# Sample scores of six of eight chains computed inside the next tile's visit, in spare PSUM columns

## The chip, the cores and the metric

The kernel runs on one core of one Trainium2 chip. The metric is the device time of one execution in microseconds (us). TensorE (PE in the profile, its weight loads PEld) multiplies matrices into PSUM, which has eight banks of 512 fp32 columns; VectorE (DVE) and ScalarE (ACT) read PSUM and do the elementwise work; GpSimd (POOL) and SyncE (SP, which issues most transfers) work beside them.

## The reference

One inference step of a two-layer decoder of width 2048: layer 0 is a gated linear recurrence (HGRN2), layer 1 a sliding-window attention with 32 query heads of 64, 4 key heads and a sink per query head. Each layer has an input projection, the mixer with a SiLU gate, an output projection and a LayerNorm. It serves one prompt (16 learned tokens and 256) and 8 samples of 8 tokens, which share the weights. The change touches only the attention of the samples:

```python
keys = jnp.concatenate([cache_k.astype(jnp.float32), k], axis=1)      # 128 cached + 8 own, per sample
s = jnp.einsum('bnqhgd,bnshd->bnhgqs', q, k) * SWA_SCALE
s = jnp.where(mask[None, :, None, None], s, -jnp.inf)
m = jnp.maximum(jnp.max(s, axis=-1, keepdims=True), sink)
p = jnp.exp(s - m)
p = p / (jnp.sum(p, axis=-1, keepdims=True) + jnp.exp(sink - m))
```

## The kernel before

**The stream of projections.** All projections of both layers are one stream of tiles of 128 output columns. A tile has 16 steps of three matmuls: weights are split into a high part (whi, a cast on ScalarE, L170) and a remainder (wlo, a subtraction on VectorE, L181), and each step multiplies low by high, high by low and high by high (L236 to L238). Four steps share one loaded chunk of weights, which is split seven chunks ahead. In layer 1 the stream runs over 2 key tiles, 2 value tiles, 16 query tiles (pj_q), 16 gate tiles (pj_g) and the output projection (y, yr).

**Side work by steps.** Everything else is written as Python generators that run beside the stream while the program is built. After each step `Stream.step` lets at most two waiting generators run on; a generator's `yield n` means: go on n steps later. So the order of instructions on every engine is fixed when the program is built, and a `yield` is a place in the order, not a time. Each engine works through its own list in order.

**A query tile's chain.** When query tile j is projected, `query_chain` undoes the folded LayerNorm (un on VectorE, L930 and L932, then qf on ScalarE, L934), splits the result into qh (ScalarE, L289) and ql (VectorE, L290), copies the samples' part into qs (GpSimd, L1090), waits ten steps and makes visit j.

**A visit.** `visit(n)` first puts on TensorE, without a pause: the prompt's scores of tile n (L1136, tiles sa and sb, from the pool lv that has two banks), the value products of tile n-2 (L1150, tile ao, from the pool mm that has three banks), the samples' value products where they are due (L1157, L1162), the transposes of tile n-1's probabilities (L1169 to L1173, tiles p1 and p2, also mm), and a transpose of cached keys (L1182, ck) or of sample probabilities (L1186, st) where due. One step later it spawns `softmax_chain(n)` and copies what TensorE made out of PSUM on ScalarE (L1194 to L1208). The softmax chain scales and masks the scores on VectorE (sm, L1236), takes the maxima (L1238, L1240) and, in `softmax`, the statistics (L1065 to L1067), three steps later the exponentials on ScalarE (L1070, L1071), and three steps after these the sums and the normalisation on VectorE (L1073 to L1076). Visit n+1 needs its result.

**The samples.** They are done in eight chains (q, u): key head q = 0 to 3, half u of the samples. The table `plan` gives each its visits: with n = 4q + 3 + u, cached keys are loaded in visit n-1 (SP, L1220 and L1223), transposed and copied to kzs in visit n ("keys", L1182 and L1204), and the finished probabilities are transposed in visit n+2 ("trans", L1186) and multiplied with the values in visit n+3 ("out"); for q = 3 the last two are somewhat earlier. In visit n, four steps after the copies (and after the next load, where there is one), `sample_scores` takes two banks of lv (ssa, ssb) and puts 16 small matmuls on TensorE (L1258): per group of 32 rows the 128 cached keys, then the 64 own keys, for each half of the rows. The profile shows each as two. One step later VectorE scales and masks them (sms, L1266), takes the maximum (L1268), and the same `softmax` follows. The scores of the next tile take the same two banks of lv.

Of the kernel before, what the change touches and what calls it, by code (L numbers as in the profile page):

```python
# [21 lines left out]
F32 = mybir.dt.float32  # L22
# [7 lines left out]
P = 128  # L30
D = 2048
KT = D // P
# [218 lines left out]
def hybrid_trunk(tc, x_prompt, x_sample, state_hgrn, cache_k, cache_v, meta, w_in0, lb_logits, norm_w, w_out0,  # L251
                 w_in1, sinks, w_out1, ln_g, ln_b, masks, consts, sinks_s,
                 y_prompt, y_sample, st_p, st_s, kp_out, vp_out, ks_out, vs_out, dbg=None, stage=9):
    nc = tc.nc
# [4 lines left out]
    with es:  # L259
# [9 lines left out]
        lv = pool("lv", 2, space=PSUM)  # L269
# [5 lines left out]
        def pm(name):  # L275
            return mm.tile([P, 512], F32, tag="mm", name=name)
# [665 lines left out]
        L = {"att": 0, "ngate": 0, "nq": 0}  # L942
# [118 lines left out]
        def softmax(stat, parts, sink):  # L1061

            n = len(parts)
            mxs, nmx, sks, rsum = (stat[:, c * n:(c + 1) * n] for c in range(4))
            nc.vector.tensor_tensor(mxs, mxs, sink, op=ALU.max)  # L1065
            nc.vector.tensor_scalar(nmx, mxs, -1.0, None, op0=ALU.mult)
            nc.vector.tensor_tensor(sks, sink, mxs, op=ALU.subtract)  # L1067
            yield 3
            for c, pt in enumerate(parts):
                nc.scalar.activation(pt, pt, AF.Exp, bias=nmx[:, c:c + 1], accum_out=rsum[:, c:c + 1])  # L1070
            nc.scalar.activation(sks, sks, AF.Exp)  # L1071
            yield 3
            nc.vector.tensor_tensor(rsum, rsum, sks, op=ALU.add)  # L1073
            nc.vector.reciprocal(rsum, rsum)
            for c, pt in enumerate(parts):
                nc.vector.tensor_scalar(pt, pt, rsum[:, c:c + 1], None, op0=ALU.mult)  # L1076
# [23 lines left out]
        plan = {}  # L1100
        for q in range(4):
            for u in range(2):
                n = 4 * q + 3 + u
# [9 lines left out]
        def visit(n, qq=None):  # L1113
            ap = L["ap"]
            todo = plan.get(n, {})
# [4 lines left out]
            if n < KT:  # L1120
# [3 lines left out]
                pa = [lv.tile([P, 512], F32, tag="lv", name=f"s{c}{n}") for c in "ab"]  # L1124
                for own in range(2):
                    t0 = 0 if own == 0 else 128
                    for i, (a, b) in enumerate(((ql, kh), (qh, kl), (qh, kh))):
                        for h in range(2):
                            r = halves2[h]
                            if own == 0:  # L1130
                                o, w, ks = (256, 0)[h], 144, b[r, 0:144]
                            elif h == 0:
                                o, w, ks = 0, 256, b[r, :].rearrange("p (a k) -> p a k", a=2)[:, :, 0:128]
                            else:
                                o, w, ks = 144, 256, b[r, 16:272]
                            nc.tensor.matmul(pa[h][:, o:o + w], a[r, t0:t0 + 128], ks, start=i == 0,  # L1136
                                             stop=i == 2, tile_position=(64 * h, 0), skip_group_check=True)
            po = None
            j2 = n - 2
            if j2 >= 0:  # L1140
                po = pm(f"ao{j2}")
            if 0 <= j2 < KT:
                vs = slice(64 * (j2 // 4), 64 * (j2 // 4) + 64)
                t1, t2 = L["t1", j2], L["t2", j2 % 2]
                for v in ("vm1", "vm2", "vm0"):
                    for h in range(2):
                        o, w, l, t = {"vm1": (0, 256, L[v], t1[:, 256 * h:256 * h + 256]),
                                      "vm2": (128, 128, L[v], t2[:, 128 * h:128 * h + 128]),
                                      "vm0": (0, 128, L["vm0"][:, h], t2[:, 256:384])}[v]
                        nc.tensor.matmul(po[halves2[h], o:o + w], l[:, vs], t, start=v == "vm1", stop=v != "vm1",  # L1150
                                         tile_position=(0, 64 * h), skip_group_check=True)
            if "out" in todo:
                q, u = todo["out"]
# [5 lines left out]
                for i in range(4):  # L1159
                    for h in range(2):  # L1160
                        c = 256 * h + 32 * i
                        nc.tensor.matmul(po[halves2[h], 256 + 32 * i:288 + 32 * i], cv[:, i, :], ts[:, c:c + 32],  # L1162
                                         start=False, stop=i == 3, tile_position=(0, 64 * h), skip_group_check=True)
            j = n - 1
            if 0 <= j < KT:
                sm = L["p", j]
                p1, p2 = pm(f"p1_{j}"), pm(f"p2_{j}")
                for h in range(2):
                    nc.tensor.transpose(p1[:, 256 * h:256 * h + 128], sm[:, 256 + 160 * h:384 + 160 * h], ident)  # L1169
                    nc.tensor.transpose(p1[:, 256 * h + 128:256 * h + 256], sm[:, 544 * h:544 * h + 128], ident)  # L1170
                for h in range(2):
                    nc.tensor.transpose(p2[:, 128 * h:128 * h + 128], sm[:, 544 * h + 128:544 * h + 256], ident)
                nc.tensor.transpose(p2[0:32, 256:384], sm[:, 384:416], ident)  # L1173
            px = None
            for kind in ("keys", "trans"):
                if kind in todo:
                    q, u = todo[kind]
# [11 lines left out]
            if n < KT:  # L1189

                g = softmax_chain(n, pa)
                st.spawn(g, next(g))
            if 0 <= j2 < KT:
                nc.scalar.copy(L["oT"][:, j2, 0:256], po[:, 0:256])  # L1194
            if 0 <= j < KT:
# [6 lines left out]
            if "keys" in todo:  # L1202
                q, u = todo["keys"]
# [5 lines left out]
            if "out" in todo:  # L1209
                yield 2  # L1210
                q, u = todo["out"]
# [3 lines left out]
            if "load" in todo:  # L1215
                yield 1 if "out" in todo else 3
                q, u = todo["load"]
# [4 lines left out]
                cv = ap.tile([P, 4, 64], F32, tag="cv", name=f"cv{q}_{u}")  # L1222
                nc.sync.dma_start(cv, cache_v[0, 4 * u:4 * u + 4, :, q, :].rearrange("b s d -> s b d"))  # L1223
                L["cd", u], L["cv", u] = cd, cv
            if "keys" in todo:
                yield 4
                yield from sample_scores(*todo["keys"])

        def softmax_chain(n, pa):
            ap = L["ap"]  # L1230

            sm = ap.tile([P, 1088], F32, tag="sm", name=f"sm{n}")
            stat = ap.tile([P, 16], F32, tag="stat", name=f"stat{n}")
            for h in range(2):
                m0 = 0 if h else 656
                nc.vector.scalar_tensor_tensor(sm[:, 400 * h:400 * h + 400], pa[h][:, 0:400], 0.125,  # L1236
                                               L["cst"][:, m0:m0 + 400], op0=ALU.mult, op1=ALU.add)
            nc.vector.tensor_reduce(stat[:, 0:2], sm[:, 256:544].rearrange("p (h k) -> p h k", h=2), axis=AX.X,  # L1238
                                    op=ALU.max)
            nc.vector.tensor_reduce(stat[:, 2:4], sm.rearrange("p (h k) -> p h k", h=2)[:, :, 0:256], axis=AX.X,  # L1240
                                    op=ALU.max)
            sink4 = ap.tile([P, 2, 2], F32, tag="sink4", name=f"sink4_{n}")
            nc.gpsimd.tensor_copy(sink4, L["sk"][:, 2 * n:2 * n + 2].unsqueeze(1).to_broadcast([P, 2, 2]))
            parts = [sm[:, 256:400], sm[:, 400:544], sm[:, 0:256], sm[:, 544:800]]
            yield from softmax(stat, parts, sink4.rearrange("p a h -> p (a h)"))
            L["p", n] = sm

        def sample_scores(q, u):

            ap = L["ap"]  # L1250
            knz, qs = L["knz", q], L["qs", q]
            ps = [lv.tile([P, 512], F32, tag="lv", name=f"ss{c}{q}_{u}") for c in "ab"]
            for own in range(2):
                for i in range(4):
                    for h in range(2):
                        r = halves2[h]
                        o, w = ((0, 64)[h], 128) if not own else ((128, 0)[h], 64)
                        nc.tensor.matmul(ps[h][32 * i:32 * i + 32, o:o + w], qs[r, 4 * u + i],  # L1258
                                         knz[r, :] if own else L["kzs", u][r, i], start=True, stop=True,
                                         tile_position=(64 * h, 32 * i), skip_group_check=True)  # L1260
            yield 1
            sm = ap.tile([P, 384], F32, tag="sms", name=f"sms{q}_{u}")
            stat = ap.tile([P, 16], F32, tag="stats", name=f"stats{q}_{u}")
            for h in range(2):
                for w, m0, o in ((128, 408, (0, 64)[h]), (64, 536 + 64 * u, (128, 0)[h])):
                    nc.vector.scalar_tensor_tensor(sm[:, 192 * h + o:192 * h + o + w], ps[h][:, o:o + w], 0.125,  # L1266
                                                   L["cst"][:, m0 - 8:m0 - 8 + w], op0=ALU.mult, op1=ALU.add)
            nc.vector.tensor_reduce(stat[:, 0:2], sm.rearrange("p (h k) -> p h k", h=2), axis=AX.X, op=ALU.max)  # L1268

            def rest():  # L1270
                yield from softmax(stat, [sm[:, 192 * h:192 * h + 192] for h in range(2)],
                                   L["sks"][:, 2 * q:2 * q + 2])
                L["sp", q, u] = sm
            st.spawn(rest())
# [306 lines left out]
```

## Time and profile before

| | us |
|---|---|
| median of 3 runs | 1149.99 (1149.36 to 1150.09) |
| the profiled execution | 1149.73 |
| its span, first to last instruction | 1147.7 |
| PE busy in the span | 1133.9 |
| DVE busy | 835.4 |
| ACT busy | 616.2 |
| query tiles' visits 0 to 15, first score matmul of each | 741.23 to 900.90 |

The mean granted clock of TensorE in the span is 0.997 of full speed. A matmul's row lasts longer than the time to the next one, since matmuls overlap in the array; the cost of one is read from the starts. In a timeline's row stand the start, the duration, engine, line, operation, output and inputs, shape and, in brackets, how long the engine had been idle and for what.

### The profile page before, as it was taken

To read this page: it belongs to the slowest core of one execution; us is meant where nothing else is said; L and a number is where in the kernel's file an instruction comes from. 1 tells how busy PE (TensorE), PEld (TensorE's weight loads), DVE (VectorE), ACT (ScalarE), POOL (GpSimd) and SP (SyncE) were. 2 spreads that over 40 slices of the span, in tenths; PEclk is the share of its full clock that TensorE was granted. 3 is DMA by queue.
4 is the path that set the end of the run, shared out by engine and by line. 5 is a ranking of instruction groups with operands and counts; after the bars stand their busy time and mean duration, and the time that the engine had idled before them with its cause. 6 is when DMAs were issued, how large, how long until landed. Compare 5 with 4: busy or idle time off the path is not lost.

```text
span 1147.7 us, 26283 instructions
## 1 busy us (share of the span) xinstructions
PE 1133.9 (99%) x10152; PEld 1102.8 (96%) x10152; DVE 835.4 (73%) x2093; ACT 616.2 (54%) x1773; POOL 257.2 (22%) x349
## 2 busy tenths in 40 slices
PE   9999999999999999999999999999999999999996
PEld 8999999999999999999999999998999999999995
DVE  4866678667687666786669876577877767787756
ACT  5654455554555544554545545566667655555531
POOL 3121222221122212122234332100000011155410
PEclk9999999999999999999999999999999999999998
DMA  9655565455564555654555555653443535555572
GB/s 252 193 148 152 149 186 143 137 163 149 157 184 119 145 158 145 184 153 132 148 148 147 147 147 161 197 139 107 121 122 103 145 103 160 145 145 147 165 203 92
DMA packets 323005, 173.39 MB, mean 151 GB/s; under 512 B 19232, under 2 KB 317664, under 8 KB 322848
## 3 DMA queue, kind: packets, MB, share of 16 engines
q1 hardware_dynamic: 320784, 166.98, 52.5%
q0 software_dynamic: 1344, 4.20, 1.4%
q8 instruction: 80, 1.31, 0.5%
q10 hardware_dynamic: 752, 0.52, 0.1%
q14 instruction: 45, 0.37, 0.1%
HBM read 158.88 MB, written 14.42 MB: 151 GB/s over the span
## 4 chain that ended last, share of the span: by engine, by line
PE 94%; DVE 3%; ACT 1%; DMA 1%; issue 0%; SPq 0%; DVEq 0%
PE pj_g L236 7%; PE pj_g L237 7%; PE pj_g L238 7%; PE pj_q L236 6%; PE pj_q L237 6%; PE pj_q L238 6%; PE pj_z L238 3%; PE pj_z L237 3%; PE pj_z L236 3%; PE pj_i L236 3%; PE pj_f L236 3%; PE pj_i L238 3%; PE pj_f L237 3%; PE pj_i L237 3%; PE pj_f L238 3%; PE yr L1434 3%
## 5 line engine op out<-in xcount | busy, mean ns | idle before, releaser
L236 PE MATMUL pj_q<-xh,wlo_q 128*128 128x336 f32 (+1 forms) x512 | 162.8, 318 | 0.0
L236 PE MATMUL pj_g<-xh,wlo_g 128*128 128x336 f32 (+1 forms) x512 | 161.9, 316 | 0.0
L237 PE MATMUL pj_g<-xl,whi_g 128*128 128x336 f32 (+1 forms) x512 | 160.6, 314 | 0.0
L237 PE MATMUL pj_q<-xl,whi_q 128*128 128x336 f32 (+1 forms) x512 | 160.5, 313 | 0.0
L238 PE MATMUL pj_g<-xh,whi_g 128*128 128x336 f32 (+1 forms) x512 | 160.3, 313 | 0.0
L238 PE MATMUL pj_q<-xh,whi_q 128*128 128x336 f32 (+1 forms) x512 | 160.3, 313 | 0.0
L181 DVE TENSOR_TENSOR wlo_g<-raw_g,whi_g 128x512 fp32r<-128x512 f32 x128 | 128.8, 1039 | 0.4
L236 PEld LDWEIGHTS pj_q<-xh,wlo_q 128*128 128x128 f32 x512 | 96.7, 189 | 1.7 <-DVE wlo_q L181 0.3
L237 PEld LDWEIGHTS pj_q<-xl,whi_q 128*128 128x128 f32 x512 | 96.8, 189 | 0.7
L236 PEld LDWEIGHTS pj_g<-xh,wlo_g 128*128 128x128 f32 x512 | 96.7, 189 | 0.2
L237 PEld LDWEIGHTS pj_g<-xl,whi_g 128*128 128x128 f32 x512 | 96.8, 189 | 0.0
L238 PEld LDWEIGHTS pj_q<-xh,whi_q 128*128 128x128 f32 x512 | 96.5, 189 | 0.0
L238 PEld LDWEIGHTS pj_g<-xh,whi_g 128*128 128x128 f32 x512 | 96.5, 189 | 0.0
L181 DVE TENSOR_TENSOR wlo_q<-raw_q,whi_q 128x512 fp32r<-128x512 f32 x128 | 86.3, 685 | 4.6 <-ACT whi_q L170 4.1
L236 PE MATMUL pj_i<-xh,wlo_i 128*128 128x336 f32 x256 | 84.0, 328 | 0.0
L236 PE MATMUL pj_z<-oh,wlo_z 128*128 128x336 f32 x256 | 81.5, 318 | 0.0
L236 PE MATMUL pj_f<-xh,wlo_f 128*128 128x336 f32 x256 | 81.5, 318 | 0.0
L238 PE MATMUL pj_z<-oh,whi_z 128*128 128x336 f32 x256 | 81.2, 317 | 0.0
L237 PE MATMUL pj_f<-xl,whi_f 128*128 128x336 f32 x256 | 81.1, 317 | 0.0
L238 PE MATMUL pj_i<-xh,whi_i 128*128 128x336 f32 x256 | 81.0, 316 | 0.0
L237 PE MATMUL pj_z<-ol,whi_z 128*128 128x336 f32 x256 | 81.0, 316 | 0.0
L238 PE MATMUL pj_f<-xh,whi_f 128*128 128x336 f32 x256 | 80.8, 316 | 0.0
(404 smaller groups left out, 3183.9 us busy)
## 6 DMA issues: line engine op xcount, KB each, us to landing
raw_q<-in_swa_w_in_dram SPq DMA_DIRECT2D x32, 512.0 KB
raw_g<-in_swa_w_in_dram SPq DMA_DIRECT2D x32, 512.0 KB
raw_f<-in_hgrn_w_in_dram SPq DMA_DIRECT2D x30, 512.0 KB
raw_q<-in_hgrn_w_in_dram SPq DMA_DIRECT2D x30, 512.0 KB
raw_g<-in_hgrn_w_in_dram SPq DMA_DIRECT2D x30, 512.0 KB
raw_i<-in_hgrn_w_in_dram SPq DMA_DIRECT2D x30, 512.0 KB
raw_z<-in_hgrn_w_out_dram SPq DMA_DIRECT2D x24, 512.0 KB
raw_y<-in_swa_w_out_dram SPq DMA_DIRECT2D x24, 512.0 KB
```

What stands on the lines that cost most here:

```text
L181: e.nc.vector.tensor_tensor(lo, t.pop(("raw", kc)), hi.bitcast(F32), op=ALU.subtract)
L236: nc.tensor.matmul(ps, lo[:, kk, :], xh, start=first, stop=False)
L237: nc.tensor.matmul(ps, hi[:, kk, :], xl, start=False, stop=False)
L238: nc.tensor.matmul(ps, hi[:, kk, :], xh, start=False, stop=last)
L1434: nc.tensor.matmul(t["ps", b], x[:, cs], w, start=b < 2 and k == 0 and i == 0, stop=k == KT - 1 and i == len(pairs) - 1)
```

## The change

The products of a chain and the reading of them become two functions, `sample_products` and `sample_scores`, and the products get their place in PSUM as an argument. For the six chains whose following visit still has a score tile (keys in visits 3, 4, 7, 8, 11 and 12) the products move from the middle of a projection tile into the next visit, 4, 5, 8, 9, 12 and 13: there they stand on TensorE behind the prompt's scores and ahead of the value products. They take no banks of their own. The cached keys' products go to columns 384 to 511 of the visit's ao and p2 tiles, the own keys' to columns 400 to 463 of sa and sb; for that p2 is allocated before p1 and before the products. Their masks, maximum and softmax follow one step later, right behind the first part of tile n's softmax chain. The two last chains (visits 15 and 16) keep the old way. The visits of load, keys, trans and out are as before, so the probabilities are wanted at the same visit as before.

```diff
-            po = None
+            po = p2 = None
             j2 = n - 2
             if j2 >= 0:
                 po = pm(f"ao{j2}")
+            j = n - 1
+            if 0 <= j < KT:
+                p2 = pm(f"p2_{j}")
+
+            late = plan.get(n - 1, {}).get("keys") if n < KT else None
+            if late:
+                late_src = (po[:, 384:512], p2[:, 384:512], pa[0][:, 400:464], pa[1][:, 400:464])
+                sample_products(*late, late_src)
...
-                p1, p2 = pm(f"p1_{j}"), pm(f"p2_{j}")
+                p1 = pm(f"p1_{j}")
...
                 g = softmax_chain(n, pa)
                 st.spawn(g, next(g))
+            if late:
+                sample_scores(*late, late_src)
...
-            if "keys" in todo:
+            if "keys" in todo and n + 1 >= KT:
                 yield 4
-                yield from sample_scores(*todo["keys"])
+                q, u = todo["keys"]
+                ps = [lv.tile([P, 512], F32, tag="lv", name=f"ss{c}{q}_{u}") for c in "ab"]
+                src = (ps[0][:, 0:128], ps[1][:, 0:128], ps[0][:, 128:192], ps[1][:, 128:192])
+                sample_products(q, u, src)
+                yield 1
+                sample_scores(q, u, src)
...
-        def sample_scores(q, u):
-
-            ap = L["ap"]
+        def sample_products(q, u, dst):
+
             knz, qs = L["knz", q], L["qs", q]
-            ps = [lv.tile([P, 512], F32, tag="lv", name=f"ss{c}{q}_{u}") for c in "ab"]
             for own in range(2):
                 for i in range(4):
                     for h in range(2):
                         r = halves2[h]
-                        o, w = ((0, 64)[h], 128) if not own else ((128, 0)[h], 64)
-                        nc.tensor.matmul(ps[h][32 * i:32 * i + 32, o:o + w], qs[r, 4 * u + i],
+                        nc.tensor.matmul(dst[2 * own + h][32 * i:32 * i + 32, :], qs[r, 4 * u + i],
                                          knz[r, :] if own else L["kzs", u][r, i], start=True, stop=True,
                                          tile_position=(64 * h, 32 * i), skip_group_check=True)
-            yield 1
+
+        def sample_scores(q, u, src):
+
+            ap = L["ap"]
             sm = ap.tile([P, 384], F32, tag="sms", name=f"sms{q}_{u}")
             stat = ap.tile([P, 16], F32, tag="stats", name=f"stats{q}_{u}")
             for h in range(2):
-                for w, m0, o in ((128, 408, (0, 64)[h]), (64, 536 + 64 * u, (128, 0)[h])):
-                    nc.vector.scalar_tensor_tensor(sm[:, 192 * h + o:192 * h + o + w], ps[h][:, o:o + w], 0.125,
+                for w, m0, o, p in ((128, 408, (0, 64)[h], src[h]), (64, 536 + 64 * u, (128, 0)[h], src[2 + h])):
+                    nc.vector.scalar_tensor_tensor(sm[:, 192 * h + o:192 * h + o + w], p, 0.125,
                                                    L["cst"][:, m0 - 8:m0 - 8 + w], op0=ALU.mult, op1=ALU.add)
```

More of the change, by code (lines that the diff above doesn't have):

```diff
@@ L1163, in visit @@
                                          start=False, stop=i == 3, tile_position=(0, 64 * h), skip_group_check=True)
-            j = n - 1
             if 0 <= j < KT:
                 sm = L["p", j]
-                p1, p2 = pm(f"p1_{j}"), pm(f"p2_{j}")
+                p1 = pm(f"p1_{j}")
                 for h in range(2):
```

## The prediction

> **What bounds the kernel now.** I read the page first, then the list of TensorE's waits, then TensorE's timeline over the attention stage (741 to 925 us), and last VectorE's and ScalarE's timelines there.
>
> ```profile
> span 1147.7 us, 26283 instructions
> PE 1133.9 (99%) x10152; PEld 1102.8 (96%) x10152; DVE 835.4 (73%) x2093; ACT 616.2 (54%) x1773; POOL 257.2 (22%) x349
> ...
> PE sa L1136 <- DVE sms L1266: 0.5, 1, 0.5
> ```
>
> TensorE is never short of work: in the attention stage it waits for another compute engine once, when tile 4's scores (sa, sb) want the two banks that sample chain (0,0) still holds. So a change pays only by taking issue time off TensorE, or a wait. The profiled execution took 1149.73 us, its span 1147.7; the median of the runs shown is 1149.99, 0.26 more. I make the sum on 1149.73 and add 0.26.
>
> TensorE around that first sample chain and the fourth visit:
>
> ```profile
> 775.35 0.31 PE L238 MATMUL pj_q<-xh,whi_q 128*128 128x322 f32 x1
> 775.59 0.29 PE L1258 MATMUL ssa<-kzs,qs 64*32 64x128 f32 x1
> ...
> 775.93 0.22 PE L1258 MATMUL ssb<-knz,qs 64*32 64x64 f32 x1
> 776.08 0.42 PE L236 MATMUL pj_q<-xh,wlo_q 128*128 128x322 f32 x1
> 776.34 0.30 PE L237 MATMUL pj_q<-xl,whi_q 128*128 128x322 f32 x1
> ...
> 779.59 0.31 PE L238 MATMUL pj_q<-xh,whi_q 128*128 128x322 f32 x1
> 780.39 0.30 PE L1136 MATMUL sa<-kzh,ql 64*128 64x144 f32 x1 [0.49 <-DVE sms L1266]
> ...
> 781.25 0.28 PE L1136 MATMUL sb<-kzl,qh 64*128 64x256 f32 x1
> 781.29 0.27 PE L1136 MATMUL sa<-kzh,qh 64*128 64x256 f32 x1
> 781.37 0.28 PE L1136 MATMUL sb<-kzh,qh 64*128 64x256 f32 x1
> 781.57 1.09 PE L1150 MATMUL ao<-t,vm 128*64 128x256 f32 x12
> ```
>
> Durations overlap, so I go by starts. From 776.34 to 779.59 lie 22 projection matmuls, 0.148 us each. Around the sample products, 775.35 to 776.34 is 0.99 us where two such steps would be 0.295.
>
> **The change part by part.**
>
> *Six blocks of products leave the projections.* Each frees 0.99 - 0.295 = **0.695 us**.
>
> *The same products enter a visit, between the scores and the first value product (ao).* From first to last they take 0.34 (775.59 to 775.93). What the trace lacks is the step from the scores into them and from them into ao. The step into them lies between 0.04 (one score to the next, 781.25 to 781.29) and 0.24 (projection to products); I take 0.20, what the last score needs before an instruction of another shape (781.37 to 781.57), since the products too have another shape. The step out lies between 0.01 (32 products in 0.34) and 0.24; I take 0.15 (775.93 to 776.08), the only exit from products there is. The 0.20 from scores to ao goes. Added: 0.20 + 0.34 + 0.15 - 0.20 = **0.49** (0.19 to 0.62). Net **0.205 us for each chain, 1.23 for six** (0.4 to 3.0).
>
> The Trainium skill, "TensorEngine Tiling (Array Packing)", Tiling Modes, says that changing the tiling mode drains TensorE while another tile of one mode does not. Scores (64x128), products (64x32) and ao (128x64) are three modes, so by it the low end of 0.04 is out. Here the trace agrees: 0.24 against 0.148 at such a switch.
>
> *The wait at the fourth visit goes.* An undisturbed visit:
>
> ```profile
> 758.34 0.33 PE L1136 MATMUL sa<-kzh,ql 64*128 64x144 f32 x1
> ...
> 802.04 0.33 PE L1136 MATMUL sa<-kzh,ql 64*128 64x144 f32 x1
> ...
> 824.42 0.31 PE L238 MATMUL pj_q<-xh,whi_q 128*128 128x322 f32 x1
> 824.66 0.33 PE L1136 MATMUL sa<-kzh,ql 64*128 64x144 f32 x1
> ...
> 825.34 0.28 PE L1136 MATMUL sb<-kzh,qh 64*128 64x256 f32 x1
> ...
> 846.01 0.33 PE L1136 MATMUL sa<-kzh,ql 64*128 64x144 f32 x1
> ...
> 889.98 0.33 PE L1136 MATMUL sa<-kzh,ql 64*128 64x144 f32 x1
> ```
>
> Last projection to last score: 824.42 to 825.34, 0.92; in visit 4, 779.59 to 781.37, 1.78. The stall is **0.86 us** (two banks, each waited for), more than the 0.5 listed. The chain takes no score banks of its own now, so it goes. Asked for sooner, too, is the key load of visit 4, for which nothing waited so far:
>
> ```profile
> 765.88 2.19 SPq L1220 DMA_DIRECT2D cd<-in_cache_swa_k_dram  x2
> ...
> 775.83 1.13 SPq L1220 DMA_DIRECT2D cd<-in_cache_swa_k_dram  x2
> ```
> ```profile
> 771.46 0.66 PE L1182 MATMUL ck<-ident,cd 128*128 128x128 f32 x4 [0.28 <-DMA cd<-in_cache_swa_k_dram]
> ```
>
> Visit 3's load was there 3.4 us after its issue (768.07 to 771.46), 0.28 late. Visit 4's, at the same place on SP's queue, is issued by 776.96, and its transposes come at 781.4 at the earliest (779.14, worked out below, + 0.68 scores + 0.49 products + 1.09 ao): 4.4 us later. I cost it at nothing, and at 0.3 if that cover is gone.
>
> *What is late next: the pair VectorE and ScalarE.* Tile n+1's scores need ql, at the end of a closed chain: scores read (sm), statistics, exponentials on ScalarE, one weight cast, qh, then VectorE's ql, weight remainders (wlo), normalisation, unfolding (un), the next sm.
>
> ```profile
> 757.65 0.42 DVE L290 TENSOR_TENSOR ql<-qf,qh 128x256 fp32r<-128x256 f32 x1 [2.21 <-ACT qh L289]
> ...
> 779.83 0.41 DVE L1266 SCALAR_TENSOR_TENSOR sms<-ssa,masks 128x128 f32<-128x128 f32 x2
> ...
> 781.54 1.29 DVE L181 TENSOR_TENSOR wlo_q<-raw_q,whi_q 128x512 fp32r<-128x512 f32 x2
> ...
> 826.34 0.15 DVE L1073 TENSOR_TENSOR stats<-stats 128x2 f32<-128x2 f32 x1
> ...
> 827.20 0.57 DVE L1236 SCALAR_TENSOR_TENSOR sm<-sa,masks 128x400 f32<-128x400 f32 x1
> ...
> 839.89 0.57 DVE L1236 SCALAR_TENSOR_TENSOR sm<-sa,masks 128x400 f32<-128x400 f32 x1
> ...
> 842.40 0.15 DVE L1067 TENSOR_TENSOR stat<-sink,stat 128x4 f32<-128x4 f32 x1
> ...
> 844.84 0.42 DVE L290 TENSOR_TENSOR ql<-qf,qh 128x256 fp32r<-128x256 f32 x1 [1.69 <-ACT qh L289]
> 845.18 0.69 DVE L181 TENSOR_TENSOR wlo_q<-raw_q,whi_q 128x512 fp32r<-128x512 f32 x1
> ...
> 847.12 1.29 DVE L181 TENSOR_TENSOR wlo_q<-raw_q,whi_q 128x512 fp32r<-128x512 f32 x2
> ...
> 849.31 0.57 DVE L1236 SCALAR_TENSOR_TENSOR sm<-sa,masks 128x400 f32<-128x400 f32 x1
> ```
> ```profile
> 833.30 0.60 ACT L170 CAST whi_q<-raw_q 128x512 fp32r<-128x512 f32 x1
> 833.81 0.40 ACT L289 CAST qh<-qf 128x256 fp32r<-128x256 f32 x1
> ...
> 836.32 0.46 ACT L1070 ACTIVATE sms<-sms,stats 128x192 f32<-128x192 f32 x1 [1.59 <-DVE stats L1066]
> ...
> 837.31 0.60 ACT L170 CAST whi_q<-raw_q 128x512 fp32r<-128x512 f32 x1
> ...
> 844.41 0.39 ACT L289 CAST qh<-qf 128x256 fp32r<-128x256 f32 x1
> ```
>
> Counted in steps from a visit (a step is three projection matmuls), the pauses in the code put the exponentials of its tile at step 4, those of the chain at 5, qh at 6, the normalisations at 7 and 8. So in a visit that carries a chain (a late visit) the chain's masks, maximum and statistics lie on VectorE while it waits for ScalarE: 1.71 us (779.83 to 781.54) and one wlo (0.69 in the 845.18 row), 2.40. ScalarE's stretch there is 842.40 to 844.41, 2.01 without a cast; plus the cast 0.51 (833.30 to 833.81), the chain's exponentials 0.99 (836.32 to 837.31) and 0.43 from qh to ql (844.41 to 844.84): 3.94. The 2.40 are hidden; the 0.99 on ScalarE and the chain's normalisation, 0.86 (826.34 to 827.20), are not.
>
> The late visit from sm to sm: 2.51 to the last statistic (839.89 to 842.40) + 3.94 + 0.34 (ql, 844.84 to 845.18) + 1.94 (845.18 to 847.12: wlo, normalisation) + 0.86 + 2.19 (847.12 to 849.31: two wlo, un) = **11.78**. Without a chain and with the cast: 9.42 (839.89 to 849.31) + 0.51 = 9.93.
>
> Now the two clocks. *TensorE:* tile 4's scores start at 779.59 + 0.24 - 0.695 = 779.14. Before, visits 8 to 10 took 846.01 - 824.66 = 21.35; with one block less and two entries more, 21.63. Tile 6 is due at 800.77. *VectorE:* the normalisation ends at 779.83, then two wlo and un (2.19): sm(4) at 782.02, sm(5) at 793.80, ql(6) starts 6.45 later (2.51 + 3.94), 800.25. Scores start no sooner than 0.69 after ql's start (757.65 to 758.34, where TensorE did not wait): 800.94. So tile 6 waits **0.17 us**. Behind it stand all projections, and the 0.17 is lost in full. Then sm(6) is at 805.58, sm(13) seven visits on, three late and four not (35.34 + 39.72): 880.64; ql(14) allows tile 14 from 887.78. TensorE is due at 800.94 + 87.94 (802.04 to 889.98) - 4 x 0.205 = 888.06. No second wait. Bounds of this term: 0, and 2 us (an error of 0.4 in each of five late visits).
>
> Not on the path: the chain's masks leave the four banks at about 2.51 + 0.9 after sm (797.2 in visit 5), over 3 us before the next visit's first product; po's and p2's earlier allocation takes banks emptied a visit ago; the last two chains keep their old place, and no score tile comes behind them.
>
> **Sum:** -1.23 - 0.86 + 0.17 = -1.92. Profiled 1147.8, median 1149.99 - 1.92 = **1148.1 us**. Its own range: the bounds of the products give a gain of 1.1 (0.4 + 0.86 - 0.17), and 2.2 where ql sets the end (887.78 against 889.98); with the spread of the runs shown (0.63 below their median, 0.10 above) 1147.2 to 1149.0.
>
> **The rivals.**
>
> *A, slower: VectorE and ScalarE become the pace.* The one visit of before that holds the reading of one chain and the rest of another is 827.20 to 839.89, 12.69, not 11.78. If late visits are that long: sm(13) is 782.02 + 5 x 12.69 + 4 x 9.93 = 885.19, ql allows tile 14 from 892.33, 2.35 later than 889.98: **1152.3**. It turns from gain to loss at 12.22 for a late visit. For it: 0.44 is all that separates my estimate from that point. Against it: the 12.69 hold a wait for the chain's exponentials that lies behind the main normalisation, whereas now those run ahead of it.
>
> *B, faster: the switches are cheap.* With 0.19 added rather than 0.49, TensorE gains 3.0 + 0.86; but ql(14) allows tile 14 no sooner than 887.78, a gain of 2.2, unless late visits are about 0.35 shorter too; then 1149.99 - 3.9 = **1146.1**. For: the products use other banks and half the rows each, so they may slip in early. Against: every switch in the trace costs some 0.09.
>
> *C, the change hardly does what it says:* the products cost the same at the new place (0.62, net 0.07 each), and ql waits eat some of the 0.86: -0.4 - 0.86 + 0.5 = **1149.2**.
>
> **How the numbers follow.** A measurement of this kernel can tell about 0.2%, 2.3 us, from no change. Forecast 0.50, A 0.10, B 0.20, C 0.20. Faster by over 2.3 us: B and the upper edge of the forecast, 0.26. Slower by over 2.3: A's worse half and what it leaves out, 0.09. Within: 0.65. The range takes in C, B's milder half and A's milder half: 1146.6 to 1150.8.
>
> **What would show it.** Right: no wait of sa for sms; six times no products among the projections; scores-to-ao 0.69 us (0.20 + 0.34 + 0.15) in visits 4, 5, 8, 9, 12, 13; sm to sm about 11.8 in them; a short gap ahead of tile 6's scores. Wrong: products-to-ao above 0.25, sm to sm above 12.2, TensorE waiting for ql before tiles 6, 10 and 14, or a time outside 1147.2 to 1149.0.

## The result and the profile after

The changed kernel takes **1162.71 us** (median of 5 runs), the kernel before 1149.93 in the same rounds: ratio 1.0112, 95% interval 1.0096 to 1.0128. It is slower by 1.1%, where 1148.1 and no slower than 1150.8 were forecast. One of the five runs, of 2236.01 us, was a slow one and is left out of the ratio. The profiled execution took 1162.71 us with a span of 1160.6, 12.9 more than the span before.

The page and the list of waits of the changed kernel (who waited for whom: us in total, times, longest):

```profile
span 1160.6 us, 26290 instructions
PE 1137.7 (98%) x10152; PEld 1106.6 (95%) x10152; DVE 835.6 (72%) x2093; ACT 615.1 (53%) x1773; POOL 257.2 (22%) x349
PE 88%; DVE 6%; ACT 4%; DMA 1%; issue 1%; SPq 0%; DVEq 0%
...
ACT oT L1203 <- DVE sms L1280: 37.0, 6, 6.7
...
PE sa L1136 <- DVE ql L290: 8.0, 4, 2.1
...
PE pj_g L236 <- ACT qf L934: 0.8, 1, 0.8
PE pj_q L236 <- ACT qf L934: 0.8, 1, 0.8
```

No engine is given more work than before: VectorE is busy 835.6 us against 835.4, ScalarE 615.1 against 616.2, and TensorE, 3.8 us busier, has the same 10152 matmuls, some at a lower clock (last section). What is new is waiting. Six times, once in each visit that carries a sample chain, ScalarE's first copy, oT out of the ao bank, waits 5.5 to 6.7 us for VectorE's sms. In the kernel before it waited for TensorE alone; its list and the same place in its visit 4:

```profile
ACT oT L1194 <- PE ao L1162: 16.3, 6, 3.5
ACT oT L1194 <- PE ao L1150: 6.6, 4, 2.6
```
```profile
783.14 0.37 ACT L1194 COPY oT<-ao 128x256 f32<-128x256 f32 x1
...
784.31 0.57 ACT L1204 COPY kzs<-ck 128x512 f32<-128x512 f32 x1
```

And TensorE, which never waited for ql before, waits for it 8.0 us, and 1.6 more at the start of two projection tiles. There the list names ScalarE's qf, but TensorE goes on just behind a weight remainder (wlo, done at 849.68 + 0.69 = 850.37) that stands on VectorE behind the chain's statistics:

```profile
849.68 0.69 DVE L181 TENSOR_TENSOR wlo_q<-raw_q,whi_q 128x512 fp32r<-128x512 f32 x1
...
850.52 0.39 PE L236 MATMUL pj_q<-xh,wlo_q 128*128 128x322 f32 x1 [0.82 <-ACT qf L934]
```

It is the chunk that this tile uses first: a tile takes its last chunk first (`ks[-1:] + ks[:-1]` in the kernel), so that one is split four chunks ahead and not seven. The wait for sms ahead of tile 4's scores is gone.

The fourth visit on TensorE, with the products in their new place:

```profile
779.78 0.28 PE L1136 MATMUL sb<-kzh,qh 64*128 64x256 f32 x1
779.99 0.29 PE L1269 MATMUL ao<-kzs,qs 64*32 64x128 f32 x1
...
780.33 0.22 PE L1269 MATMUL sb<-knz,qs 64*32 64x64 f32 x1
780.48 1.09 PE L1158 MATMUL ao<-t,vm 128*64 128x256 f32 x12
...
792.15 0.30 PE L1136 MATMUL sa<-kzh,ql 64*128 64x144 f32 x1 [2.09 <-DVE ql L290]
```

The products cost what the sum said: 0.21 in, 0.34 through, 0.15 out (0.69 forecast, 0.70 measured). The loss appears one visit later, where tile 5's scores stand still for ql. Why ql is late is on the two other engines. First VectorE, then ScalarE, in the same visit:

```profile
782.44 0.57 DVE L1250 SCALAR_TENSOR_TENSOR sm<-sa,masks 128x400 f32<-128x400 f32 x1
...
785.29 0.15 DVE L1067 TENSOR_TENSOR stat<-sink,stat 128x4 f32<-128x4 f32 x1
785.37 0.28 DVE L1280 SCALAR_TENSOR_TENSOR sms<-ao,masks 128x128 f32<-128x128 f32 x1
...
791.58 0.42 DVE L290 TENSOR_TENSOR ql<-qf,qh 128x256 fp32r<-128x256 f32 x1 [3.82 <-ACT qh L289]
...
796.91 0.57 DVE L1250 SCALAR_TENSOR_TENSOR sm<-sa,masks 128x400 f32<-128x400 f32 x1
```
```profile
785.68 0.37 ACT L1203 COPY oT<-ao 128x256 f32<-128x256 f32 x1 [6.14 <-DVE sms L1280]
785.95 0.59 ACT L1208 COPY t<-p 128x512 f32<-128x512 f32 x1
786.43 0.39 ACT L1209 COPY t<-p 128x256 f32<-128x256 f32 x1
...
787.33 0.56 ACT L934 ACTIVATE qf<-un_q,gb_q 128x320 f32<-128x320 f32 x1
787.79 0.40 ACT L1070 ACTIVATE sm<-sm,stat 128x144 f32<-128x144 f32 x1
...
791.16 0.39 ACT L289 CAST qh<-qf 128x256 fp32r<-128x256 f32 x1
```

TensorE had written ao by 781.6 (780.48 + 1.09), but ScalarE copies it at 785.68, just after VectorE's read of the same bank (785.37 + 0.28). Both only read, and different columns. Behind oT stand, in ScalarE's order, the copies of p1, p2 and kzs, then qf, then the exponentials, which begin at 787.79, 2.4 us after the statistics they need. So the visit is 14.47 us from sm to sm (782.44 to 796.91), where 11.78 was worked out. Tile 14's scores begin at 903.14, 13.2 us after the 889.98 of before, about the whole loss.

### The profile page after: what moved, and what is told of

The parts are those of the page before. It is cut to its first block, busy times and chain, and to the rows that moved or that the text cites. A ratio compares the mean times of both kernels' runs of the same rounds, so it can differ in the third digit from the quotient of the medians.

```text
span 1160.6 us, 26290 instructions
## 1 busy us (share of the span) xinstructions
PE 1137.7 (98%) x10152; PEld 1106.6 (95%) x10152; DVE 835.6 (72%) x2093; ACT 615.1 (53%) x1773; POOL 257.2 (22%) x349
## 4 chain that ended last, share of the span: by engine, by line
PE 88%; DVE 6%; ACT 4%; DMA 1%; issue 1%; SPq 0%; DVEq 0%
PE pj_g L236 7%; PE pj_g L237 7%; PE pj_g L238 7%; PE pj_q L236 5%; PE pj_q L237 5%; PE pj_q L238 5%; PE pj_z L238 3%; PE pj_z L237 3%; PE pj_z L236 3%; PE pj_i L236 3%; PE pj_f L236 3%; PE pj_i L238 3%; PE pj_i L237 3%; PE pj_f L238 3%; PE pj_f L237 3%; PE yr L1448 3%
## 5 line engine op out<-in xcount | busy, mean ns | idle before, releaser
L237 PE MATMUL pj_i<-xl,whi_i 128*128 128x336 f32 x256 | 80.8, 316 | 0.0
```

What stands on the lines that cost most here:

```text
L237: nc.tensor.matmul(ps, hi[:, kk, :], xl, start=False, stop=False)
```

## The experiments

**Theory T.** Two engines that read one PSUM bank are kept in the order of the program. The change writes VectorE's reading of ao and p2 ahead of ScalarE's copies out of the same banks, so ScalarE waits for VectorE, and its copies fall into the closed chain that sets ql. Rivals: the chain's place is too much work for VectorE and ScalarE in any order (A of the prediction), or the products are dear (P).

**1. The reading behind the copies.** Nothing else is moved.

```diff
-            if late:
-                sample_scores(*late, late_src)
             if 0 <= j2 < KT:
                 nc.scalar.copy(L["oT"][:, j2, 0:256], po[:, 0:256])
...
                 nc.scalar.copy(t2[0:32, 256:384], p2[0:32, 256:384])
+            if late:
+                sample_scores(*late, late_src)
```

> The changed kernel with one thing moved: VectorE's reading of a sample chain (masks and maximum) is written behind ScalarE's copies out of ao, p1 and p2 in the visit, not ahead of them; all products, places and steps stay. Theory T (order of readers): in the changed kernel ScalarE's first copy (oT, out of ao) waits some 6 us for VectorE's read of the same bank, and the copies then lie in the closed chain that sets ql. So here that wait is gone, late visits are about 11.8 us from sm to sm and not 14.5, TensorE waits for ql at most 0.3 us, its clock stays at 1.00, and the time is 1148.1 us (1147.2 to 1149.2). Rival A (a chain that reads its scores right behind the tile's own is too much work for VectorE and ScalarE, whatever the order of the copies): late visits stay at 12.7 or more, the time at 1152 or more. Rival P (products among the visit's matmuls are dear): 1155 or more with no wait for ql.

Measured: **1148.16 us** against 1150.07, ratio 0.9985 (0.9977 to 0.9994). That kernel's ScalarE and VectorE, visit 4 and then visits 8 to 10:

```profile
781.34 0.38 ACT L1201 COPY oT<-ao 128x256 f32<-128x256 f32 x1 [2.27 <-PE ao L1158]
...
782.66 0.26 ACT L1208 COPY t<-p 32x128 f32<-32x128 f32 x1
...
783.29 0.56 ACT L934 ACTIVATE qf<-un_q,gb_q 128x320 f32<-128x320 f32 x1
784.94 0.42 ACT L1070 ACTIVATE sm<-sm,stat 128x144 f32<-128x144 f32 x1 [1.09 <-DVE stat L1066]
```
```profile
784.89 0.28 DVE L1280 SCALAR_TENSOR_TENSOR sms<-ao,masks 128x128 f32<-128x128 f32 x1
...
825.75 0.57 DVE L1250 SCALAR_TENSOR_TENSOR sm<-sa,masks 128x400 f32<-128x400 f32 x1
...
837.53 0.57 DVE L1250 SCALAR_TENSOR_TENSOR sm<-sa,masks 128x400 f32<-128x400 f32 x1
...
849.31 0.57 DVE L1250 SCALAR_TENSOR_TENSOR sm<-sa,masks 128x400 f32<-128x400 f32 x1
```

oT now waits for TensorE alone. The copies out of ao, p1 and p2 are done by 782.9, two microseconds before VectorE reads at 784.89, so the order costs VectorE nothing either. qf is done too, and the exponentials wait for the statistics alone. Both late visits shown, 8 and 9, are 11.78 us. TensorE never waits for ql. A and P fall: the whole 12.8 us lie in the place of one call.

**2. Half of it: only oT ahead.**

```diff
-            if late:
-                sample_scores(*late, late_src)
             if 0 <= j2 < KT:
                 nc.scalar.copy(L["oT"][:, j2, 0:256], po[:, 0:256])
+            if late:
+                sample_scores(*late, late_src)
             if 0 <= j < KT:
```

> The changed kernel with only ScalarE's copy out of ao (oT) written ahead of VectorE's reading; the copies out of p1 and p2 stay behind it. T: any bank that both read makes the later one wait, so the wait goes over from oT to the first copy out of p2; out of the closed chain come only oT and the copy of p1 (about 0.27 and 0.48 us), so late visits are about 14.0 us from sm to sm, TensorE still waits for ql, and the time is about 1159.5 us (1156.5 to 1161.5). Rival Q (it is ao alone, whose reading waits): about 1148 as in the kernel with all copies ahead.

Measured: 1161.33 us against 1150.07 (ratio 1.0097, 1.0081 to 1.0112). The list of waits and ScalarE in visit 4:

```profile
ACT t L1209 <- DVE sms L1280: 20.6, 6, 4.3
...
787.01 0.37 ACT L1209 COPY t<-p 128x256 f32<-128x256 f32 x1 [3.23 <-DVE sms L1280]
```

The wait went over to the first copy out of p2, as T says and Q does not. Late visits are 13.6 to 14.1 us from sm to sm.

**3. The reading alone, in the kernel before.** The products stay where they were.

```diff
+            L["jk"] = ap1.tile([P, 1], F32, tag="jk", name="jk")
...
                 st.spawn(g, next(g))
+            if n in (4, 5, 8, 9, 12, 13):
+                nc.vector.tensor_copy(L["jk"], po[:, 0:1])
             if 0 <= j2 < KT:
```

> The kernel before, products and reading at their old places, with one added instruction in visits 4, 5, 8, 9, 12 and 13: VectorE copies one column of ao into a scratch tile (which nothing uses) right behind the tile's statistics, ahead of ScalarE's copies. T: this alone makes oT wait for VectorE, about 6 us; the copies of the visit then lie between the statistics and the exponentials: 2.4 us there, where it was 1.7 in visits 4, 8 and 12 and 0.1 in 5, 9 and 13. That is some 3.1 us for two visits against a slack of 0.3 to 1: TensorE waits about 8 us in all for ql, and where a wait is near 2 us its clock falls for some 3 us behind it, so 1158 to 1163 us. Rival (the loss needs the moved products): 1150, at most 0.7 slower for the six small instructions.

Measured: 1158.77 us against 1150.07 (ratio 1.0079, 1.0065 to 1.0092). Its list of waits:

```profile
ACT oT L1197 <- DVE jk L1195: 22.0, 6, 4.2
PE ssa L1261 <- ACT kzs L1207: 5.2, 3, 1.9
PE sa L1137 <- DVE ql L290: 2.0, 2, 1.0
```

Six one-column reads cost 8.7 us: the loss needs no moved product. The size was met, the place only in part. oT waited 3.7 us on average and not 6. ql was awaited 2.0 us and not 8, while 5.2 fell on the products, at their old place soon after kzs, which stands behind oT on ScalarE. Some 1.5 of the 8.7 are a fall of TensorE's clock behind one of these waits (last section).

**4. The control: the same read, behind the copies.**

```diff
+            L["jk"] = ap1.tile([P, 1], F32, tag="jk", name="jk")
...
                 nc.scalar.copy(t2[0:32, 256:384], p2[0:32, 256:384])
+            if n in (4, 5, 8, 9, 12, 13):
+                nc.vector.tensor_copy(L["jk"], po[:, 0:1])
```

> Control to the kernel before with one added one-column read of ao on VectorE: the same six instructions, written behind ScalarE's copies. T: the instruction itself costs 0.1 us of VectorE, ScalarE does not wait for it: 1150.1 us, at most 0.7 slower than the kernel before. Rival (the added instruction, or VectorE reading that bank at all, costs the time): 1155 or more, as with the read ahead.

Measured: 1150.06 us against 1149.95 (ratio 0.9998, 0.9988 to 1.0007). The instruction costs nothing that can be told; its place is the 8.7 us.

**5. Half the visits, as a test of the sum.**

```diff
-            if late:
+            if late and n % 4 == 0:
                 sample_scores(*late, late_src)
...
                 nc.scalar.copy(t2[0:32, 256:384], p2[0:32, 256:384])
+            if late and n % 4 == 1:
+                sample_scores(*late, late_src)
```

> The changed kernel with the reading written behind ScalarE's copies in visits 5, 9 and 13 only; in 4, 8 and 12 it stays ahead of them. T, put as a sum: the time is set by the closed chain of VectorE and ScalarE, not by TensorE's own work. Visits 4, 8 and 12 take 14.15 us from sm to sm (measured with the changed kernel: 14.47, 14.14, 14.14), visits 5, 9 and 13 11.78 (measured with all readings behind), the others 9.95. From sm(4) at 782.0 that is 3 x 14.15 + 2 x 11.78 + 4 x 9.95 = 105.8 to sm(13) at 887.8, ql(14) lets tile 14 begin 7.14 later, at 894.95, against 889.98 before: 5.0 slower, 1155.1 us (1154.0 to 1157.0), and a fall of TensorE's clock after a wait costs nothing where ql is awaited next. Rival L (loss in proportion to the waiting instructions, three of six): half of 12.8 and the full gain, 1156.5 or more with the waits spread evenly. Rival C (the falls of the clock carry the loss): the time follows their number.

Measured: 1155.69 us against 1149.95 (ratio 1.0047, 1.0031 to 1.0064), 5.7 slower. VectorE's first masks of visits 4, 5 and 6, and of 8, 9 and 10, then the first score of tile 14 on TensorE:

```profile
782.10 0.56 DVE L1252 SCALAR_TENSOR_TENSOR sm<-sa,masks 128x400 f32<-128x400 f32 x1
...
796.57 0.57 DVE L1252 SCALAR_TENSOR_TENSOR sm<-sa,masks 128x400 f32<-128x400 f32 x1
...
808.34 0.56 DVE L1252 SCALAR_TENSOR_TENSOR sm<-sa,masks 128x400 f32<-128x400 f32 x1
...
828.23 0.56 DVE L1252 SCALAR_TENSOR_TENSOR sm<-sa,masks 128x400 f32<-128x400 f32 x1
842.36 0.57 DVE L1252 SCALAR_TENSOR_TENSOR sm<-sa,masks 128x400 f32<-128x400 f32 x1
...
854.12 0.56 DVE L1252 SCALAR_TENSOR_TENSOR sm<-sa,masks 128x400 f32<-128x400 f32 x1
```
```profile
895.20 0.33 PE L1136 MATMUL sa<-kzh,ql 64*128 64x144 f32 x1
```

14.47 and 11.77, then 14.13 and 11.76: each visit has the length that its own order gives it. Tile 14's scores begin at 895.20 where the sum over the closed chain had 894.95; its 14.15 was not the mean of the three visits it named, which is 14.25, and with that the sum is 895.25. The time does not part T from L well: half of the 14.6 us between the changed kernel and experiment 1 would be 1155.4 as well, less than L's text allowed. The lengths of the visits do, since the waits are not spread evenly. C falls: there is no fall of the clock in this run (last section).

One more kernel gave no time: experiment 1 with the chain's softmax started one step later deadlocks. It was to bring late visits to 10.8 us, at 1147.9 expected; whether a shorter late visit would still gain anything is not shown.

## Why the prediction was wrong

**The products (net 0.205 us each, 1.23 in all): right**, 0.70 against 0.69 from scores to ao (0.96 in visit 5 of the changed kernel, at the lower clock).

**The stall of 0.86 at tile 4: right**, no wait for sms is left there. The key load's cover held: no new wait for cd.

**The closed chain (11.78 us for a late visit, 9.93 for others): the arithmetic was right, for another order.** Experiment 1 measures 11.77 to 11.78 and 9.95 (12.13 in visit 4, where VectorE stands 0.46 ahead of the statistics; the profile names GpSimd's copy of the sinks, but the same 0.46 stands in the changed kernel, where that copy starts at 788.12, three microseconds too late to end it, so its cause is open). In the changed kernel late visits take 14.0 to 14.5.

**The step that failed** is the sentence "The 2.40 are hidden", with what was set down under "Not on the path". I asked when the chain's masks leave the four banks for TensorE, and not who else reads them. ScalarE's copies of ao and p2 are written behind the masks, and are made to wait for them. In visit 4 it is 6.29 us from the last statistic to ql (785.29 to 791.58), where 3.94 was taken. Between the masks' read and the exponentials lie 785.68 to 787.79, 2.11 us of copies and qf, which in experiment 1 are done (781.34 to 783.85) while VectorE is busy with the scores. That makes 2.35 more in visit 4, and 2.2 to 2.4 in the late visits behind it, which carries their length over the point of 12.22 that rival A named.

**Rival A** had the place (VectorE and ScalarE become the pace) and the right point of decision, but neither the mechanism nor the size. Its 12.69 would have given 1152.3. The five late visits ahead of sm(13) measured 14.47, 14.02, 14.14, 14.01 and 14.14.

**The 0.17 us wait for ql at tile 6 did not come** in experiment 1. One wait of 0.46 for a weight remainder (wlo, done at 799.07; TensorE goes on at 799.21) is there instead, which the sum did not have. The sum with the right order, 1148.1, stands against 1148.16, and the last tenths of that are luck: from tile 0's scores to tile 14's the trace of experiment 1 has 147.16 us and that of the kernel before 148.75, a gain of 1.59 (about 1.23 + 0.86 - 0.46) and not 1.92.

The Trainium skill, "PSUM — Partial Sum Buffer", Terms, says that two engines on one bank at once collide, reads against reads included, and that the compiler back end keeps engines apart. The traces agree with the keeping apart: in the changed kernel oT is released by sms, in experiment 2 the copy of p2 is. No run here shows a collision. Each of these tiles fills a bank, so the runs do not tell whether the order is kept by bank or by tile, nor what keeps it. By that page the second reader would have been in the sum.

## What to carry to other kernels

Spare columns of a PSUM bank are not free of the bank's other users: list every engine that reads the bank, and write the reader that is ready first ahead of the one that comes late. A read that only waits its turn on one engine can hold up a whole queue on another; what stands behind the waiting instruction has to be counted. A price worked out by engine time alone holds only for the order of instructions that it assumes.

## What the hardware showed

TensorE's granted clock (the third figure from the end of each row; behind it the transfers' share and GB/s) in the changed kernel, after the waits that end at 792.15 and 806.17:

```profile
792.20:794.00 1.80, 1.80 (x46) 1.49 (x48) 1.73 (x8) 0.96 (x3) 0.00 (x0) 0.77 0.00 0
794.00:796.00 2.00, 2.00 (x14) 1.29 (x13) 1.93 (x7) 0.00 (x0) 0.00 (x0) 0.50 0.03 8
796.00:798.00 2.00, 2.00 (x15) 1.99 (x14) 1.93 (x6) 0.00 (x0) 0.00 (x0) 0.85 0.59 169
...
808.00:810.00 2.00, 2.00 (x28) 1.90 (x24) 1.93 (x7) 0.00 (x0) 0.00 (x0) 0.50 0.00 0
```

It falls to 0.50 for some 3 us after a pause of about 2 us, but not each time: after three of four such pauses here, one of four in experiment 2, one of three in experiment 3, and not after the one in experiment 5 (2.39 us, up to 791.81), whose clock in the 5 us behind it is the 1.00 of this row:

```profile
791.80:796.80 5.00, 4.99 (x76) 4.45 (x77) 4.83 (x16) 2.79 (x9) 0.00 (x0) 1.00 0.08 24
```

The Trainium skill, "TensorE: Matmul & The Clock Gate", Part 1, puts the fall behind an idle window of about 3.4 us that runs freely; here pauses of 1.9 to 2.4 us (789.75 to 792.15 the first) were enough, so that length doesn't hold in this trace. A fall takes some 1.7 us of TensorE's work (1.8 x 0.23 + 2.0 x 0.50 + 2.0 x 0.15), but where the next scores wait for ql anyway it adds little: experiment 5 shows no fall and still lost what the closed chain alone accounts for. In the changed kernel two of the three falls make a visit without a chain 10.4 us instead of 9.95 (820.87 to 831.26, 869.36 to 879.74), 0.9 us of the 12.8. Where the next scores do not wait for ql, a fall costs more: in experiment 3 tile 5's scores come 15.29 us after tile 4's (780.33 to 795.62), in the kernel before 11.82; of the 3.47 more, 1.92 are the wait for kzs, and the other 1.5 are the clock, at 0.51 and 0.62 in the 3.9 us behind it (an estimate by that difference). What decides whether a pause brings a fall stays open.
